# Second block: convolution sums in PSUM, weight halves subtracted on GpSimd, attention's gates between its parts, other lane rates

## The chip, the cores and the metric

The kernel runs on one core of a Trainium2 chip. The metric is the time of one execution on the device in microseconds (us); lower is better. The engines are called by their names; in the rows PE is TensorE (PEld its weight loads), DVE is VectorE, ACT is ScalarE, POOL is GpSimd and SP is SyncE, which only issues DMAs here.

## The reference, cut to what matters

Two layers of a first model run, then one layer of a second model, on 512 tokens of width 1024, all in float32. The part of the reference that the change touches is the second model's mixer:

```python
h = rms_norm(x, pre_norm1[l]) * (1.0 + sc1) + sh1
proj = h @ w_in[l]                       # 1024 x 7168: u_glu, q, k, v, gates
...
ua, ub = jnp.split(u_glu, 2, axis=-1)
u = ua * jax.nn.sigmoid(ub)
u = lax.conv_general_dilated(u, conv_w, ..., padding=[(30, 0)], feature_group_count=1024) + conv_b
u = jax.nn.silu(layer_norm(u, conv_ln_g, conv_ln_b))
y_conv = u @ conv_w_out + conv_b_out
...
att = causal_diff_attention(q1, q2, k1, k2, v, lam)     # 8 heads, v of width 128
y_att = (rms_norm(att, head_norm) * (1.0 - lam_init)).reshape(B, T, 1024)
g_conv, g_att = jnp.split(jax.nn.sigmoid(gate_logits), 2, axis=-1)
y = (g_conv * y_conv + g_att * y_att) @ w_o
x = x + g1 * rms_norm(y, post_norm1)
```

The convolution is causal, per channel, with 31 taps over 512 positions.

## The kernel before

**Weights and products.** All weights lie in one stream, cut into units of at most 128 x 1024 numbers in the order of use (`UNITS`). `unit` keeps three units ready; `_fetch` loads a unit into one of three `raw` buffers and `split` makes an upper half `wh` (a ScalarE copy that rounds) and a lower half `wl` = raw - wh (a VectorE subtraction, L380) from it. Some units are held in slots in place of the rings, as two tiles of 512 columns. Every product is three matmuls (`mm3`, L462 to L464): upper with upper, upper with lower, lower with upper. `fm` makes 128 output columns of a layer from a unit (24 matmuls of 512 columns); one `beat` follows each `mm3` there, and every third beat is a `tick`.

**Lanes.** Work that isn't on the main line is written as generators in lanes. At each tick a lane gains its rate as credit, and each whole credit runs one step, up to the next `yield`. `finish` runs a lane to its end at once. The Tile framework puts the instructions of TensorE, VectorE, ScalarE and GpSimd into an order of its own from the order of the program and its estimates, and adds the semaphores; DMAs keep the order written. Each engine then executes in order.

**Memory.** 78 slots of 128 x 512 float32 in SBUF (`big`) and eight banks of PSUM (`psum`) are handed out in the order in which they came free.

**The second block's mixer.** Eight pairs of GLU units give `us[i]`. `convolve(i)` starts `acc` in a slot on ScalarE and adds 30 taps on VectorE (`scalar_tensor_tensor`, L398), three to a step. After all eight, `conv_norm` (L1750 on) takes the mean, subtracts it in 8 steps, takes the reciprocal deviation (`sums` L589, `powm` on GpSimd L593, `spread` L619), and finishes the tiles `cn[i]` in 8 more. Both are in the lane `conv`. The main line runs four attention parts: q and k of two heads (four banks, 96 matmuls of 512 columns), `rope2`, v (two units). After each, `diff_attention` queues a transposing generator (L1663) and four blocks (`_diff_block`) in the lane `att`, two active at a time: scores L1691, masked copy L544, exponentials, transposes L1715, products L1723, head norm with a power on GpSimd, transposes L1741 into `ya`. A gate is one unit and its tanh; `combine` multiplies a finished `ya` with its gate. `GATES` says how many gates follow each part: none, none, none, sixteen. Then comes `finish("conv")`, and eight units of conv_w_out, which need all `cn`; when a `ya` isn't done there, `finish("att")` is called. The next stage is w_o, in halves of 256 columns.

Rates before: `conv` 0.6 during the GLU and the parts, 0.8 from part 3's end; `att` 1.0, and 1.5 from conv_w_out on.

## Time and profile before

| | us |
|---|---|
| median of three runs | 2490.43 (2488.10 to 2490.53) |
| profiled execution | 2488.26 |
| its span, first to last instruction | 2486.1 |
| TensorE busy | 2444.6 |
| VectorE busy | 1638.6 |
| ScalarE busy | 1064.8 |
| GpSimd busy | 318.7 |

The span holds 12206 matmuls and some 5900 instructions of VectorE, ScalarE and GpSimd. Matmuls overlap, and their ends are modelled, so that a busy TensorE isn't one at its peak: the number of matmuls in a stretch tells more. Idle time of an engine that doesn't set the pace costs nothing. PEclk is the share of TensorE's full clock that was granted.

### The profile page before, as it was taken

What the parts mean: (1) busy time and instruction counts of PE and PEld (TensorE: products, weight loads), DVE (VectorE), ACT (ScalarE), POOL (GpSimd) and SP (SyncE); (2) the same over time, 40 slices, a digit from 0 to 9 for tenths busy, and PEclk for the clock granted to TensorE, in tenths of its full rate; (3) what the DMA queues carried; (4) which work ended last, traced back from release to release, by engine and by line L of the source; (5) the groups of instructions that cost most, each with busy time, mean ns of one, the idle gap of its engine ahead of it and who ended that gap; (6) DMA issues with size and microseconds to landing.
All of it is one profiled execution on the core that took longest, in us unless ns stands there. A gap on an engine that the chain in (4) does not pass through costs nothing.

```text
span 2486.1 us, 32470 instructions
## 1 busy us (share of the span) xinstructions
PE 2444.6 (98%) x12206; PEld 2053.9 (83%) x12206; DVE 1638.6 (66%) x3064; ACT 1064.8 (43%) x1984; POOL 318.7 (13%) x820
## 2 busy tenths in 40 slices
PE   9999999999999999999999999999999989999998
PEld 7888888888888888888888788988887769988887
DVE  6998755444355488865677644799899675643335
ACT  6567433332234365643423223523445565634222
POOL 7923000000056054100000000000000000000000
PEclk9999999999999999999999999999999989999999
DMA  4222232222323322133466633322211113122232
GB/s 156 86 71 77 80 132 93 96 100 94 101 97 128 97 73 75 60 102 127 133 219 207 222 113 107 126 89 103 77 60 68 47 64 119 69 93 89 94 106 76
DMA packets 83677, 256.57 MB, mean 103 GB/s; under 512 B 9536, under 2 KB 10944, under 8 KB 83520
## 3 DMA queue, kind: packets, MB, share of 16 engines
q1 hardware_dynamic: 83520, 254.50, 30.2%
q8 instruction: 95, 1.56, 0.3%
q14 instruction: 62, 0.51, 0.1%
HBM read 248.18 MB, written 6.29 MB: 102 GB/s over the span
## 4 chain that ended last, share of the span: by engine, by line
PE 83%; DVE 7%; DMA 5%; ACT 2%; issue 2%; SPq 0%; POOL 0%; DVEq 0%; POOLq 0%; ACTq 0%
PE bank L462 26%; PE bank L463 26%; PE bank L464 26%; DMA slot<-in_wada_dram 4%; DVE slot L380 2%; DVE wl L380 2%; ACT slot L377 2%; DVE slot L398 2%; PE bank L1691 1%; PE bank L1723 1%; DMA raw<-in_w_dram 0%; PE bank L1194 0%; PE bank L1206 0%; DVE slot L394 0%; PE bank L1014 0%
## 5 line engine op out<-in xcount | busy, mean ns | idle before, releaser
L462 PE MATMUL bank<-slot,wh 128*128 128x512 f32 x2456 | 964.5, 394 | 7.3 <-ACT slot L377 7.3
L464 PE MATMUL bank<-slot,wl 128*128 128x512 f32 x2456 | 959.7, 392 | 2.8 <-DVE wl L380 2.8
L463 PE MATMUL bank<-slot,wh 128*128 128x512 f32 x2456 | 959.9, 391 | 0.0
L377 ACT ACTIVATE wh<-raw 128x1024 fp32r<-128x1024 f32 (+3 forms) x369 | 385.2, 1045 | 774.2 <-PE bank L463 401.8
L380 DVE TENSOR_TENSOR wl<-raw,wh 128x1024 fp32r<-128x1024 f32 (+3 forms) x369 | 450.4, 1221 | 216.9 <-ACT wh L377 214.9
L462 PEld LDWEIGHTS bank<-slot,wh 128*128 128x128 f32 x2456 | 463.5, 189 | 105.8 <-ACT slot L377 9.1
L464 PEld LDWEIGHTS bank<-slot,wl 128*128 128x128 f32 x2456 | 462.5, 188 | 102.8 <-DVE wl L380 6.0
L463 PEld LDWEIGHTS bank<-slot,wh 128*128 128x128 f32 x2456 | 463.2, 189 | 95.3 <-DVE slot L398 0.7
L380 DVE TENSOR_TENSOR slot<-bank,slot 128x512 f32<-128x512 f32 (+4 forms) x340 | 197.4, 592 | 229.3 <-PE bank L464 207.9
L377 ACT ACTIVATE slot<-slot 128x512 fp32r<-128x512 f32 (+4 forms) x378 | 207.6, 558 | 293.6 <-DVE slot L380 269.8
L380 DVE TENSOR_TENSOR slot<-slot,slot 128x512 f32<-128x512 f32 (+4 forms) x480 | 288.4, 619 | 50.2 <-ACT slot L377 47.1
L377 ACT ACTIVATE slot<-bank 128x512 f32<-128x512 f32 (+7 forms) x398 | 182.7, 475 | 128.2 <-PE bank L464 47.8
L463 PE MATMUL bank<-wl,slot 128*128 128x512 f32 (+1 forms) x480 | 180.9, 377 | 0.0
L464 PE MATMUL bank<-wh,slot 128*128 128x512 f32 (+1 forms) x480 | 180.1, 376 | 0.0
L462 PE MATMUL bank<-wh,slot 128*128 128x512 f32 (+1 forms) x480 | 179.5, 377 | 0.0
L463 PE MATMUL bank<-slot,slot 128*128 128x256 f32 (+1 forms) x624 | 178.3, 291 | 0.3 <-DVE slot L398 0.3
L464 PE MATMUL bank<-slot,slot 128*128 128x256 f32 (+1 forms) x624 | 178.3, 290 | 0.0
L398 DVE SCALAR_TENSOR_TENSOR slot<-slot,slot 128x512 f32<-128x512 f32 (+1 forms) x184 | 123.9, 689 | 81.1 <-DMA slot<-in_wada_dram 58.0
L462 PE MATMUL bank<-slot,slot 128*128 128x256 f32 (+1 forms) x624 | 176.5, 292 | 0.3 <-ACT slot L377 0.3
L398 DVE SCALAR_TENSOR_TENSOR slot<-slot,cw,slot 128x485 f32<-128x485 f32 (+28 forms) x240 | 166.6, 731 | 1.9 <-ACT slot L377 1.1
L380 DVE TENSOR_TENSOR slot<-slot,bank 128x512 f32<-128x512 f32 (+1 forms) x104 | 66.2, 644 | 128.8 <-PE bank L464 128.5
L463 PEld LDWEIGHTS bank<-slot,slot 128*128 128x128 f32 x624 | 118.9, 192 | 2.6 <-DVE slot L398 0.5
(197 smaller groups left out, 2163.2 us busy)
## 6 DMA issues: line engine op xcount, KB each, us to landing
raw<-in_w_dram SPq DMA_DIRECT2D x373, 512.0 KB, 3.3
slot<-in_wada_dram SPq DMA_DIRECT2D x96, 256.0 KB, 5.0
raw<-in_w_dram SPq DMA_DIRECT2D x32, 448.0 KB, 3.4
slot<-in_x_dram SPq DMA_DIRECT2D x16, 256.0 KB, 3.8
xd<-slot SPq DMA_DIRECT2D x16, 256.0 KB, 3.8
slot<-xd SPq DMA_DIRECT2D x16, 256.0 KB, 3.6
out_dram<-slot SPq DMA_DIRECT2D x8, 256.0 KB, 2.0
slot<-in_bc_dram SPq DMA_DIRECT2D x8, 128.0 KB, 3.1
```

Of the source, the lines that this page charges most:

```text
L377: return self.nc.scalar.activation(out=out, in_=in_, func=func, scale=scale, **kw)
L380: return (eng or self.nc.vector).tensor_tensor(out=out, in0=a, in1=b, op=op)
L398: return self.nc.vector.scalar_tensor_tensor(out=out, in0=a, scalar=s, in1=b, op0=op0, op1=op1, **kw)
L462: t.matmul(ps, ah, bh, start=start, stop=False)
L463: t.matmul(ps, ah, bl, start=False, stop=False)
L464: t.matmul(ps, al, bh, start=False, stop=stop)
L1691: nc.tensor.matmul(ps[e][:, :w], qk[s][x][rows, tn], qk[2 + s][y][rows, :w], start=i == 0, stop=i == 2)
L1723: nc.tensor.matmul(po[:, e], at[e][:, b], vv[b // 2][:, b % 2, 128 * e:128 * e + 128], start=b == 0, stop=b == n)
```

## The change

The convolution's running sum moves from a slot to a PSUM bank; at its end ScalarE copies it into a slot, and the sum over channels reads the bank. GpSimd makes the lower halves of the units of w_in_2 from the seventh on and of conv_w_out_2 (`BESIDE`). Two gates follow part 1, two part 2 and twelve part 3, in the order `GATE_ORDER`, where m < 8 are attention's gates and m >= 8 the convolution's. In a `_diff_block` the step ends move: one after both transposes, one after both products, one between the power on GpSimd and the product that reads it; `dfin` gets a third buffer. The lane `att` has the rate 1.45 throughout; `conv` gets its rate anew at each part from the steps that are left (`steps`), five ticks for the rest after part 3, and `conv_norm` sets 0.7.

```diff
-R1, R2, R3, R4, R5, R6 = 0.9, 1.0, 0.6, 0.6, 0.8, 1.5
+R1, R2, R3 = 0.9, 1.45, 0.6
...
-GATES = (0, 0, 0, 16)
+GATES = (0, 2, 2, 12)
+GATE_ORDER = (0, 1, 2, 3, 4, 5, 8, 9, 10, 11, 12, 13, 14, 15, 6, 7)
...
-    gates = [("w_in_2", 0, 0, 8, c + 128 * m, 128) for c in (6144, 5120) for m in range(8)]
+    gates = [("w_in_2", 0, 0, 8, (6144 if m < 8 else 5120) + 128 * (m % 8), 128) for m in GATE_ORDER]
...
+_SECOND = len(UNITS) - len(_units_second())
+BESIDE = {i for i, u in enumerate(UNITS) if i >= _SECOND + GLU_HELD and u[0] in ("w_in_2", "conv_w_out_2")}
...
-    def split(self, hi, lo, src, scale=None):
+    def split(self, hi, lo, src, scale=None, eng=None):
         if scale is None:
             self.act(hi, src)
-            self.sub(lo, src, hi.bitcast(F32))
+            self.sub(lo, src, hi.bitcast(F32), eng)
...
+        eng = self.nc.gpsimd if i in BESIDE else None
...
-                self.split(h, l, raw[:, c].rearrange("p (k c) -> p k c", k=n))
+                self.split(h, l, raw[:, c].rearrange("p (k c) -> p k c", k=n), eng=eng)
...
-                self.split(h[:, c], l[:, c], raw[:, c])
+                self.split(h[:, c], l[:, c], raw[:, c], eng=eng)
...
         def convolve(i):
-            acc = self.big(f"acc{i}")
+
+            acc = self.psum(f"acc{i}")
...
                 if j % 3 == 0:
+                    steps[0] -= 1
                     yield
             self.free(us[i])
-            conv.append(acc)
+            conv.append(self.big(f"conv{i}"))
+            self.act(conv[i], acc)
             if i == 1:
                 csum.append(self.big("csum"))
-                self.add(csum[0], conv[0], conv[1])
+                self.add(csum[0], conv[0], acc)
             elif i > 1:
                 self.add(csum[0], csum[0], acc)
+            self.free(acc)
...
+        steps = [80]
...
-        self.lane("conv", 1, R4)
         for part in range(4):
+
+            cl.rate = steps[0] / (16 * (4 - part) + 8 / 3 * (6 - sum(GATES[:part])))
...
-                self.lane("conv", 1, R5)
-            for m in range(sum(GATES[:part]), sum(GATES[:part + 1])):
+                cl.rate = steps[0] / 5
+            for m in GATE_ORDER[sum(GATES[:part]):sum(GATES[:part + 1])]:
                 gate(m)
         self.free(hs, self.cs2)
         self.finish("conv")
-        self.lane("att", 2, R6)
...
             self.act(at[e][:, :n + 1], pt[:, :n + 1])
             self.free(pt, pp[e])
-            yield
+        yield
...
             self.free(at[e])
-            if e == 0:
-                yield
-        fin = self.small("dfin", (128, 2), bufs=2)
+        yield
+        fin = self.small("dfin", (128, 2), bufs=3)
...
         self.powm(ss, ss, 2)
+        yield
         self.mul(ss, ss, fin)
...
         while len(conv) < 8:
             yield
+        self.lanes["conv"].rate = 0.7
```

## Rows read from the trace of the kernel before

**Rows 1.** The page: engines (busy us, share, instructions); a costly group (busy, mean ns).
```profile
PE 2444.6 (98%) x12206; PEld 2053.9 (83%) x12206; DVE 1638.6 (66%) x3064; ACT 1064.8 (43%) x1984; POOL 318.7 (13%) x820
...
L398 DVE SCALAR_TENSOR_TENSOR slot<-slot,cw,slot 128x485 f32<-128x485 f32 (+28 forms) x240 | 166.6, 731 | 1.9 <-ACT slot L377 1.1
```

**Rows 2.** Busy time by stretch: PE, PEld, DVE, ACT, POOL; PEclk; DMA share, GB/s.
```profile
1500.00:1550.00 50.00, 50.00 (x222) 41.42 (x221) 22.94 (x31) 14.76 (x21) 0.00 (x0) 1.00 0.35 111
1640.00:1720.00 80.00, 80.00 (x387) 67.31 (x386) 79.10 (x117) 25.66 (x34) 0.00 (x0) 1.00 0.33 112
...
1920.00:1940.00 20.00, 17.33 (x79) 12.84 (x77) 17.73 (x42) 9.29 (x26) 0.00 (x0) 0.91 0.16 53
1940.00:1980.00 40.00, 39.99 (x190) 30.33 (x188) 24.03 (x57) 22.92 (x56) 1.39 (x2) 1.00 0.21 72
1980.00:1990.00 10.00, 8.10 (x58) 6.18 (x56) 6.24 (x19) 7.38 (x23) 2.37 (x3) 1.00 0.02 4
1990.00:2000.00 10.00, 3.96 (x19) 2.90 (x18) 10.00 (x21) 10.00 (x19) 0.00 (x0) 0.66 0.00 0
2000.00:2010.00 10.00, 9.35 (x28) 7.25 (x29) 9.20 (x25) 7.37 (x22) 0.00 (x0) 0.66 0.38 131
2010.00:2060.00 50.00, 49.94 (x222) 37.41 (x222) 32.22 (x68) 26.24 (x61) 1.39 (x2) 1.00 0.26 92
2060.00:2070.00 10.00, 8.60 (x64) 7.40 (x63) 7.04 (x16) 7.32 (x19) 0.69 (x1) 1.00 0.36 133
...
1640.00:2000.00 360.00, 348.50 (x1821) 283.79 (x1819) 314.81 (x614) 164.80 (x368) 11.56 (x13) 0.99 0.21 73
```

**Rows 3.** TensorE's waits from 1980 to 2002: us in total, times, longest.
```profile
PE bank L1691 <- DVE slot L380: 3.6, 2, 2.7
...
PE bank L1691 <- DVE dmx L544: 0.8, 1, 0.8
```

**Rows 4.** Timeline of TensorE, 1982 to 2004: start, us, what, idle before.
```profile
1982.90 0.95 PE L589 MATMUL bank<-ones,slot 128*128 128x1 f32 x8
...
2000.65 1.65 PE L462 MATMUL bank<-slot,wh 128*128 128x512 f32 x3 [0.97 <-ACT slot L377]
```

**Rows 5.** VectorE's groups by shape from 1440 to 2100: busy us, mean ns.
```profile
L380 DVE TENSOR_TENSOR wl<-raw,wh 128x1024 fp32r<-128x1024 f32 x62 | 75.7, 1221 | 13.7 <-ACT wh L377 13.1 <-PE bank L464 0.6
L380 DVE TENSOR_TENSOR slot<-slot,slot 128x512 f32<-128x512 f32 x69 | 46.1, 688 | 0.4 <-ACT slot L377 0.2
L380 DVE TENSOR_TENSOR slot<-raw,slot 128x512 fp32r<-128x512 f32 x56 | 37.6, 687 | 13.7 <-ACT slot L377 12.1 <-PE bank L1715 1.3
...
L380 DVE TENSOR_TENSOR slot<-bank,slot 128x512 f32<-128x512 f32 x14 | 9.7, 692 | 40.2 <-PE bank L464 40.2
```

**Rows 6.** Timeline of GpSimd, 204 to 207 us.
```profile
204.42 0.45 POOL L380 TENSOR_TENSOR slot<-s_xx 128x128 f32<-128x128 f32 x1
...
206.42 0.73 POOL L380 TENSOR_TENSOR slot<-s_xx 128x256 f32<-128x256 f32 x1
```

**Rows 7.** GpSimd's groups by shape, whole span.
```profile
L593 POOL TENSOR_TENSOR dss<-dss,mhalf 128x2 f32<-128x2 f32 x16 | 13.4, 835 | 446.6 <-DVE dss L395 249.6 <-ACT djk L377 197.0
```

**Rows 8.** Timeline of VectorE and GpSimd, 755 to 760 us.
```profile
755.80 3.42 DVE L380 TENSOR_TENSOR wl<-raw,wh 128x896 fp32r<-128x896 f32 x1
...
756.36 0.30 POOL L380 TENSOR_TENSOR s_w<-slot,s_lr 128x64 f32<-128x64 f32 x1
...
758.13 1.23 POOL L380 TENSOR_TENSOR s_w<-slot,s_lr 128x64 f32<-128x64 f32 x1
```

**Rows 9.** Two lines' instructions: count, duration in ns min/median/max, first and last start.
```profile
L1168 DVE COPY slot<-slot x64: 260/270/1452, 42.8 to 1013.6; 32x128 f32<-32x128 f32 x64
...
L1248 DVE COPY slot<-bank x64: 372/384/400, 123.2 to 1069.3; 32x128 f32<-32x128 f32 x64
```

**Rows 10.** Timeline of VectorE, 1901 to 1905 us.
```profile
1901.14 3.96 DVE L398 SCALAR_TENSOR_TENSOR slot<-slot,cw,slot 128x505 f32<-128x505 f32 x6
```

## The prediction

> **What bounds the kernel now.** I read the page first. TensorE is busy 98% of the span [rows 1], so work that leaves another engine is worth nothing by itself: only stretches in which TensorE idles or runs slowly can pay. Next came the busy time by stretch. Where nothing disturbs it, TensorE issues 222 matmuls of 512 columns in 50 us, 0.225 us each [rows 2]. The second block's convolution and attention lie between about 1640 and 2070 us, and there the reader sees two different things [rows 2]. From 1640 to 1720 VectorE is full (79.1 of 80 us) while TensorE loses nothing. From 1920 on TensorE loses: 2.67 us idle at 1920 to 1940, then 1.90, 6.04 and 0.65 us in the three stretches from 1980 to 2010, and 1.40 us at 2060 to 2070. Between the two, at 1940 to 1980, VectorE is busy only 24.0 of 40 us. So the work is badly spread: too much early, too little at 1940, too much at once at 1990, where VectorE and ScalarE are both busy 10.00 of 10 us.
>
> The waits say what the big gap is: attention's score matmuls (L1691) wait for a difference on VectorE (L380), 2.7 us at the longest [rows 3]. The timeline shows the chain: the sums over partitions (L589) that conv_norm needs before its last eight steps run only at 1982.90, and conv_w_out's first matmul (L462) starts at 2000.65, after a wait for ScalarE [rows 4]. In the ten us from 2000 only 28 matmuls start, where 44 would at 0.225 us. [...]
>
> Why conv_norm is late can be counted in the code. A tick is three beats, one beat is three matmuls of 512 columns, so a tick lasts 9 x 0.225 = 2.0 us plus what the lanes put in. The convolutions take 8 x 10 = 80 steps, conv_norm 17. Ten GLU units give 26.7 ticks x 0.6 = 16 steps, four parts 64 x 0.6 = 38, sixteen gates 42.7 x 0.8 = 34: 88 of 97. The other 8 or 9 are drained by `finish("conv")`, and the late sums fit that. Attention has 4 x 32 = 128 steps; 48 + 42.7 ticks at rate 1.0 do 91, conv_w_out's 21.3 ticks at 1.5 another 32, the rest is drained at the end: the idle at 2060.
>
> **What the change can take away.** Idle at 1980 to 2010: 1.90 + 6.04 + 0.65 = 8.6 us. Low clock after it: 16 missing matmuls x 0.225 = 3.6 us less the 0.65 us already counted, 3.0 us. At 1920 to 1940: 2.67 us idle and, with the granted clock at 0.91, 0.09 x 20 = 1.8 us, together 4.5 us; VectorE was nearly full there (17.7 of 20). At 2060: 1.4 us. Sum 17.5 us.
>
> **The change part by part.** *Rates and gates.* By the same count the convolution has 64 steps left at part 0 and 64 + 16 ticks to do them in, rate 0.8, and stays there; in part 3 some 4 steps remain, done in 5 ticks; conv_norm's 17 steps at 0.7 take 24 of the 27 ticks left in the last twelve gates. So `finish("conv")` finds nothing. Attention gets 16 x 3 + 5.3 x 2 + 32 = 90.7 ticks x 1.45 = 131 steps for 128, and is done before conv_w_out. The number of matmuls and of weight transfers stays. Thus the gap, its low clock and the idle at 2060 go, if the other engines follow.
>
> *GpSimd takes the lower halves.* 58 units from the seventh GLU unit on; of these, 42 whole ones and 16 half tiles of attention's values fall between 1640 and 2000. VectorE loses 42 x 1.221 + 16 x 0.687 = 62 us there [rows 5]. Undelayed, GpSimd's instructions with two inputs take 0.45 us for 128 columns and 0.73 us for 256 [rows 6], 2.2 ns a column, so 0.73 + 768 x 0.0022 = 2.4 us for 1024. Without any fixed part it would be 4 x 0.73 = 2.9 us; I take 2.4. A unit lasts TensorE 24 x 0.225 = 5.4 us and is fetched two units ahead, so either value is hidden; the cover is gone above 5.4 us. [...]
>
> GpSimd's queue is in order, and its power for the head norm (835 ns [rows 7]) now stands behind a 2.4 us subtraction. VectorE's next product waits for it, and behind that product all of VectorE. The new yield puts the product about two lane steps later, 2 / 1.45 ticks x 2 us = 2.8 us against up to 3.2: at worst 0.4 us for each of 16 blocks. conv_norm's own power has no such yield: up to 2.4 us once, in front of its `spread`.
>
> *Sharing with VectorE.* At 755.80 a VectorE subtraction of 896 columns took 3.42 us, where 1.221 x 896 / 1024 gives 1.07. Meanwhile GpSimd's instructions ran at their normal 0.30 us, up to one that took 1.23 us in the same form when VectorE at last ran [rows 8]. So one excludes the other. A copy on VectorE from SBUF has a median of 270 and a maximum of 1452 ns; the same from PSUM, in the same stages, 384 and 400 [rows 9]. Hence the convolution's instructions, with the sum in PSUM, should run beside GpSimd, and those with two SBUF inputs should not. [...]
>
> Its price here: in 1640 to 2000 VectorE is busy 314.8 us. Less 62, plus at most the 32.2 us that it does at 2010 to 2060 and that now comes earlier [rows 2]: 285 us. The stretch shrinks to about 360 - 18 = 342 us, so 57 us are free. GpSimd would be busy 42 x 2.4 + 16 x 1.3 = 121 us, 35% of it. VectorE comes to some 104 runs of instructions with two SBUF inputs there (16 rope groups, 3 runs in each of 16 attention blocks, about 32 in conv_norm, 8 combines); 104 x 0.35 x half of 2.4 us = 44 us. Bounds: nothing, and all 121. I take 44: VectorE is then busy 329 of 342 us, which just fits.
>
> *Sums in PSUM.* No row shows VectorE writing PSUM. Reading it costs nothing: 512 columns take 692 ns from PSUM and 688 ns from SBUF [rows 5]. Bounds: none, or the loss of the overlap by which six convolution instructions of 0.73 us [rows 1] take 3.96 us, 0.65 us apart [rows 10]: 0.08 x 240 = 19 us of VectorE. I take none, since reading shows none. Eight ScalarE copies lie beside units of 5.4 us, hidden: ScalarE was under half busy at 1920 to 1940. One bank of eight is gone, so while four banks hold q and k, attention turns over three, not four.
>
> *New waits.* Head norms 16 x 0.4 x 0.35 = 2.2 us, conv_norm's power 2.4 x 0.35 = 0.8 us: 3.0 us. Lower bound 0; the upper ends are the rivals.
>
> Net 17.5 - 3.0 = 14.5 us. The profiled execution took 2488.3 us, 2.2 us more than its span; it becomes 2473.8. The median of the runs is 2490.4, 2.1 us above the profiled one, so **2476 us**.
>
> **The rivals.** *VectorE still sets the pace.* If each of the 58 GpSimd instructions costs VectorE 1.2 us, not 0.76, that is 70 us against 57 free: 13 us too many, the drain comes back in part, gain 4, 2486 us. For it: VectorE was held over 2 us in [rows 8]. Against: half of its time is convolution, which should be immune. *A bank too few, slower.* With three banks, each of the 32 score steps takes the banks of the step before, about one lane step earlier, and TensorE, in order, waits until VectorE's masked read is done. The nearest row is the 0.8 us wait for dmx [rows 3]; 32 x 0.8 = 26 us against 17.5 gained: 2498 us. It decides above 17.5 / 32 = 0.55 us a step. For it: VectorE is nearly full. Against: matmuls of the parts can be put in front of the scores. *Everything fits.* No new waits; the low clock of 1990 to 2000 goes too (at most 0.34 x 10 = 3.4 us, not counted above because TensorE was mostly idle), and that stretch's 19 small matmuls shrink from 3.96 / 19 = 0.21 us each to the 8.10 / 58 = 0.14 us of the ten us before, 1.3 us [rows 2]: 17.5 + 4.7 = 22.2 us, 2468 us.
>
> **How the numbers follow.** Forecast 0.55, everything fits 0.10, VectorE sets the pace 0.20, a bank too few 0.15. The range reaches from 2 us below the best case, whose clock terms are estimates, to midway between the two bad ones: 2466 to 2492; the forecast's own is 2470 to 2482. About 5 us (0.2%) can be told from no change: faster takes the forecast, the best case and under half of the pace rival, 0.73; same 0.12; slower 0.15, the bank rival.
>
> **What would show it.** Right: conv_norm's second sums (L589) well before the last gate, no idle of several us and no low clock before conv_w_out, VectorE even between 1700 and 2000, 66 GpSimd subtractions of 2 to 3 us, products with two SBUF inputs above their 688 ns, convolution instructions still near 0.73 us. Wrong: GpSimd subtractions above 5 us; convolution instructions stretched too; conv_w_out's first matmuls still waiting for ScalarE; score matmuls waiting for VectorE time after time.

## The result, and the profile after

The changed kernel takes 2520.82 us (median of four runs, 2519.07 to 2525.02) against 2489.26 us for the kernel before in the same comparison: a ratio of 1.0129, 95% interval 1.0116 to 1.0142. It is slower, by 31.6 us, and lies above the range of 2466 to 2492 and above the slow rival's 2498. The profiled execution took 2519.07 us, with a span of 2517.3.

Three lines of the page of the changed kernel: the engines, the convolution's group, GpSimd's new group.

```profile
PE 2454.1 (97%) x12206; PEld 2062.8 (82%) x12206; DVE 1636.5 (65%) x2998; ACT 1069.4 (42%) x1992; POOL 463.2 (18%) x886
...
L404 DVE SCALAR_TENSOR_TENSOR bank<-slot,cw,bank 128x493 f32<-128x493 f32 (+14 forms) x240 | 173.7, 735 | 7.0 <-ACT bank L383 2.9
L386 POOL TENSOR_TENSOR wl<-raw,wh 128x1024 fp32r<-128x1024 f32 x50 | 127.1, 2547 | 221.7 <-ACT wh L383 212.3
```

Against [rows 1] TensorE has the same 12206 matmuls, and a tap of the convolution costs VectorE 735 ns in place of 731. GpSimd's subtraction takes 2.55 us where 2.4 was estimated. So the parts have about the forecast prices. But VectorE's total hardly falls, 1638.6 to 1636.5 (1646.8 in the run below that leaves the subtractions on VectorE): nearly all of what it gave away it got back in longer instructions.

Most of the loss has one place. It lies between the first matmul of the first part's q and k and the first of w_o: 1689.7 to 2066.1 before, 1693.0 to 2096.0 after, nearly the same work (1881 and 1893 matmuls). The next two fences are these two stretches (columns as in [rows 2]), first of the kernel before, then of the changed one.

```profile
1689.70:2066.10 376.40, 362.79 (x1881) 291.19 (x1880) 312.13 (x649) 190.82 (x447) 12.95 (x15) 0.98 0.21 72
```

```profile
1693.00:2096.00 403.00, 370.67 (x1893) 300.80 (x1892) 315.00 (x602) 199.13 (x467) 130.73 (x71) 0.94 0.20 71
```

It is 26.6 us longer, of the 31.2 us by which the span grew; 3.3 us lie ahead of it, where the runs below differ by more among themselves (the stretch starts at 1689.2 to 1700.6), and 1.3 behind it. TensorE idles 403.0 - 370.7 = 32.3 us against 13.6, which is 18.7 us; the other 7.9 us are busy time, 370.7 against 362.8, at a granted clock of 0.94 against 0.98. "The stretch" below is always this one, read in the same way.

Stretches of 20 us in the changed kernel show where, same columns:

```profile
1800.00:1820.00 20.00, 20.00 (x107) 16.73 (x106) 6.04 (x12) 8.79 (x23) 8.73 (x8) 1.00 0.16 54
1820.00:1840.00 20.00, 12.33 (x60) 9.51 (x59) 18.29 (x36) 10.04 (x25) 7.53 (x3) 0.76 0.44 157
1840.00:1860.00 20.00, 16.48 (x110) 14.72 (x110) 19.52 (x46) 6.90 (x25) 1.23 (x2) 0.90 0.00 1
...
1900.00:1920.00 20.00, 13.44 (x61) 9.39 (x59) 19.96 (x43) 9.90 (x24) 8.39 (x4) 0.81 0.45 158
...
2000.00:2020.00 20.00, 20.00 (x81) 15.21 (x79) 4.90 (x21) 7.30 (x21) 4.08 (x3) 0.80 0.00 1
```

The gap at the drain is gone: while the second sums of conv_norm run (2007.4 to 2011.7) TensorE is busy all the time, where [rows 2, 4] had 6.04 us idle in 10. The granted clock there is still low, 0.80. In place of the gap stand new stalls at the ends of the parts' q and k. VectorE is little used in one stretch (6.04 of 20 us) and nearly full in the next two (18.29, then 19.52): the evenness that the forecast wanted did not come.

TensorE's waits in the changed kernel, 1440 to 2140 (total, times, longest), are what the forecast named as a sign that it is wrong, score matmuls that wait for VectorE. Line numbers have moved: here L1703 are the scores, L551 is the masked read (it writes `dmx`), L1727 the transposes behind the difference (L404), L1735 the products, L1753 the last transposes, L469 to L471 `mm3`, L386 the plain two-input instructions and L383 ScalarE's. In the other runs the same lines lie a few numbers off.

```profile
PE bank L1703 <- DVE dmx L551: 16.8, 6, 5.9
PE bank L1727 <- DVE slot L404: 4.9, 2, 3.2
PE bank L1753 <- ACT slot L383: 3.7, 3, 1.9
PE bank L1735 <- ACT slot L383: 3.1, 3, 1.5
```

The longest one in the timeline, TensorE first, then VectorE, then GpSimd:

```profile
1824.57 0.39 PE L471 MATMUL bank<-wh,slot 128*128 128x512 f32 x1
1824.88 2.40 PE L1703 MATMUL bank<-slot,slot 64*128 64x128 f32 x18
1833.13 1.21 PE L1703 MATMUL bank<-slot,slot 64*128 64x128 f32 x6 [5.86 <-DVE dmx L551]
1836.04 1.65 PE L1703 MATMUL bank<-slot,slot 64*128 64x512 f32 x3 [1.69 <-DVE dmx L551]
1837.62 0.58 PE L469 MATMUL bank<-slot,slot 128*128 128x256 f32 x1
```

```profile
1820.25 0.69 DVE L386 TENSOR_TENSOR slot<-bank,slot 128x512 fp32r<-128x512 f32 x1 [1.05 <-ACT slot L383]
1822.22 10.65 DVE L386 TENSOR_TENSOR slot<-slot,slot 128x256 f32<-128x256 f32 x9 [1.28 <-ACT slot L383]
1832.79 0.28 DVE L551 CUSTOM_DVE_ANT_0 slot<-bank,slot 128x128 f32<-128x128 f32 x1
```

```profile
1817.17 2.38 POOL L386 TENSOR_TENSOR wl<-raw,wh 128x1024 fp32r<-128x1024 f32 x1 [7.14 <-ACT wh L383]
1824.12 7.53 POOL L386 TENSOR_TENSOR wl<-raw,wh 128x1024 fp32r<-128x1024 f32 x3 [4.58 <-ACT wh L383]
```

Right behind part 2's q and k TensorE has eighteen score matmuls in a row, three steps' worth, and then needs the banks that the masked reads (L551) must free. These stand on VectorE behind nine rope instructions, which take 10.65 us while three GpSimd subtractions run back to back for 7.53 us. The matmuls of v (L469, 256 columns) are behind the scores in TensorE's queue, so nothing fills the wait. It looks like a tale of GpSimd; the experiments say otherwise, since the stalls stay when GpSimd's part is undone.

### The profile page after: what moved, and what is told of

It reads as the page before. It is cut to its first block, busy times and chain, and to the rows that moved or that the text cites. A ratio compares the mean times of both kernels' runs of the same rounds, so it can differ in the third digit from the quotient of the medians.

```text
span 2517.3 us, 32504 instructions
## 1 busy us (share of the span) xinstructions
PE 2454.1 (97%) x12206; PEld 2062.8 (82%) x12206; DVE 1636.5 (65%) x2998; ACT 1069.4 (42%) x1992; POOL 463.2 (18%) x886
## 4 chain that ended last, share of the span: by engine, by line
PE 76%; DVE 11%; DMA 6%; issue 2%; ACT 2%; POOL 2%; SPq 1%; DVEq 0%; POOLq 0%; ACTq 0%
PE bank L469 23%; PE bank L470 23%; PE bank L471 23%; DVE slot L386 4%; DMA slot<-in_wada_dram 4%; DVE wl L386 2%; DVE slot L404 2%; ACT slot L383 2%; PE bank L1703 1%; DMA raw<-in_w_dram 1%; POOL s_w L386 1%; POOL slot L386 1%; PE bank L1735 1%; DVE bank L404 1%; DVE slot L400 0%
## 5 line engine op out<-in xcount | busy, mean ns | idle before, releaser
L469 PE MATMUL bank<-slot,wh 128*128 128x512 f32 x2456 | 964.3, 394 | 5.5 <-ACT slot L383 5.5
L471 PE MATMUL bank<-slot,wl 128*128 128x512 f32 x2456 | 960.5, 392 | 4.3 <-DVE wl L386 4.3
L383 ACT ACTIVATE wh<-raw 128x1024 fp32r<-128x1024 f32 (+3 forms) x369 | 385.1, 1044 | 744.0 <-PE bank L470 356.1
L471 PEld LDWEIGHTS bank<-slot,wl 128*128 128x128 f32 x2456 | 462.9, 188 | 106.2 <-DVE wl L386 9.3
L469 PEld LDWEIGHTS bank<-slot,wh 128*128 128x128 f32 x2456 | 463.3, 189 | 101.6 <-ACT slot L383 5.9
L386 DVE TENSOR_TENSOR wl<-raw,wh 128x1024 fp32r<-128x1024 f32 (+3 forms) x319 | 389.2, 1221 | 204.1 <-ACT wh L383 202.5
L386 DVE TENSOR_TENSOR slot<-bank,slot 128x512 f32<-128x512 f32 (+4 forms) x340 | 197.5, 591 | 242.5 <-PE bank L471 208.6
L383 ACT ACTIVATE slot<-slot 128x512 fp32r<-128x512 f32 (+4 forms) x378 | 207.3, 558 | 315.5 <-DVE slot L386 291.2
L386 DVE TENSOR_TENSOR slot<-slot,slot 128x512 f32<-128x512 f32 (+4 forms) x473 | 299.5, 652 | 62.9 <-ACT slot L383 58.9
L383 ACT ACTIVATE slot<-bank 128x512 f32<-128x512 f32 (+7 forms) x406 | 187.5, 476 | 131.9 <-PE bank L471 47.4
L404 DVE SCALAR_TENSOR_TENSOR slot<-slot,slot 128x512 f32<-128x512 f32 (+1 forms) x184 | 129.9, 723 | 89.3 <-DMA slot<-in_wada_dram 60.6
L469 PE MATMUL bank<-slot,slot 128*128 128x256 f32 (+1 forms) x624 | 180.7, 296 | 2.9 <-ACT slot L383 2.2
L471 PE MATMUL bank<-slot,slot 128*128 128x256 f32 (+1 forms) x624 | 181.0, 293 | 0.0
L470 PE MATMUL bank<-slot,slot 128*128 128x256 f32 (+1 forms) x624 | 180.2, 293 | 0.3 <-DVE slot L404 0.3
L469 PE MATMUL bank<-wh,slot 128*128 128x512 f32 (+1 forms) x480 | 179.9, 379 | 0.5 <-ACT slot L383 0.5
L471 PE MATMUL bank<-wh,slot 128*128 128x512 f32 (+1 forms) x480 | 180.3, 376 | 0.0
L404 DVE SCALAR_TENSOR_TENSOR bank<-slot,cw,bank 128x493 f32<-128x493 f32 (+14 forms) x240 | 173.7, 735 | 7.0 <-ACT bank L383 2.9
L386 POOL TENSOR_TENSOR wl<-raw,wh 128x1024 fp32r<-128x1024 f32 x50 | 127.1, 2547 | 221.7 <-ACT wh L383 212.3
L386 DVE TENSOR_TENSOR slot<-slot,bank 128x512 f32<-128x512 f32 (+1 forms) x111 | 71.0, 646 | 133.9 <-PE bank L471 128.3
```

What stands on the lines that cost most here:

```text
L383: return self.nc.scalar.activation(out=out, in_=in_, func=func, scale=scale, **kw)
L386: return (eng or self.nc.vector).tensor_tensor(out=out, in0=a, in1=b, op=op)
L404: return self.nc.vector.scalar_tensor_tensor(out=out, in0=a, scalar=s, in1=b, op0=op0, op1=op1, **kw)
L469: t.matmul(ps, ah, bh, start=start, stop=False)
L470: t.matmul(ps, ah, bl, start=False, stop=False)
L471: t.matmul(ps, al, bh, start=False, stop=stop)
```

## The experiments

All ratios are to the kernel before in the same session, with the 95% interval. "Behind" is the time from w_o's first matmul to the end of the span, 420.0 us before and 421.3 after. No run that does the whole work was measured faster than the kernel before.

| run | ratio | stretch | behind |
|---|---|---|---|
| the whole change | 1.0129 [1.0116, 1.0142] | 403.0 | 421.3 |
| undo_gpsimd | 1.0110 [1.0095, 1.0125] | 400.2 | 421.3 |
| undo_psum | 1.0272 [1.0255, 1.0289] | 439.9 | 424.5 |
| rates_gates | 1.0082 [1.0067, 1.0097] | 393.5 | 421.9 |
| own_bank | 1.0141 [1.0126, 1.0157] | 403.8 | 423.4 |
| att_slow | 1.0046 [1.0021, 1.0071] | 377.1 | 426.2 |
| rates_gates_slow | 1.0020 [1.0001, 1.0038] | 369.3 | 428.0 |
| rates_gates_slow5 | 1.0031 [1.0020, 1.0043] | 372.2 | 428.8 |
| att_mid | 1.0133 [1.0118, 1.0149] | 403.8 | 422.0 |
| conv_end | 1.0008 [0.9989, 1.0027] | 374.5 | 420.0 |
| gates_only | 1.0024 [1.0008, 1.0040] | 379.4 | 422.7 |
| steps_only | 1.0036 [1.0023, 1.0048] | 381.2 | 423.0 |
| gates_gpsimd | 1.0097 [1.0081, 1.0112] | 399.9 | 420.4 |
| half_taps_before | 0.9955 [0.9942, 0.9967] | 361.4 | 420.5 |
| half_taps_after | 1.0104 [1.0090, 1.0118] | 396.6 | 422.4 |
| pause | 1.0182 [1.0168, 1.0196] | 416.3 | 425.0 |
| crowd | 1.0011 [1.0002, 1.0020] | 370.4 | 427.5 |
| width_one | 1.0092 [1.0076, 1.0108] | 396.0 | 425.8 |
| width_three | 1.0058 [1.0043, 1.0074] | 388.1 | 423.0 |

### The parts undone one by one

**undo_gpsimd**: the whole change, lower halves on VectorE.

```diff
-        eng = self.nc.gpsimd if i in BESIDE else None
+        eng = None
```

> The changed kernel, with the lower halves back on VectorE. Exclusion theory (VectorE's instructions with two SBUF inputs, rope first, are held by rows of GpSimd subtractions, and the scores behind them): the waits for dmx, 16.8 us, and most of the low clock go, 2485 to 2495 us. Bank theory (the sum in PSUM takes a bank from attention and ties the start of each convolution to that bank's earlier user): the waits for dmx and the gaps of the convolution stay, 2510 us or more. Density theory (attention at 1.45 is too close for VectorE): 2510 us or more too.

Measured 1.0110. The loss stays, so GpSimd is not its main cause; the 0.19% (4.7 us) between the two runs is at the edge of the noise, for their intervals overlap. TensorE still waits for the masked reads, now also in front of the matmuls of v (1640 to 2140):

```profile
PE bank L1703 <- DVE dmx L551: 6.9, 4, 4.4
PE bank L469 <- DVE dmx L551: 6.6, 3, 3.2
```

In the stretch, VectorE by shape (busy us, mean ns), first this run, then the whole change, then GpSimd in the whole change:

```profile
L386 DVE TENSOR_TENSOR slot<-slot,slot 128x512 f32<-128x512 f32 x53 | 35.4, 683 | 2.2 <-ACT slot L383 2.1
...
L386 DVE TENSOR_TENSOR slot<-slot,slot 128x256 f32<-128x256 f32 x32 | 12.0, 419 | 0.0
```

```profile
L386 DVE TENSOR_TENSOR slot<-slot,slot 128x512 f32<-128x512 f32 x53 | 44.1, 849 | 0.6
L386 DVE TENSOR_TENSOR slot<-slot,slot 128x256 f32<-128x256 f32 x32 | 21.0, 696 | 5.0 <-ACT slot L383 4.9
...
L386 DVE TENSOR_TENSOR dss<-dss,dfin 128x2 f32<-128x2 f32 x16 | 10.0, 627 | 4.7 <-POOL dss L600 4.5
```

```profile
L386 POOL TENSOR_TENSOR wl<-raw,wh 128x1024 fp32r<-128x1024 f32 x38 | 98.3, 2592 | 146.6 <-ACT wh L383 137.2 <-PE bank L1703 9.4
L386 POOL TENSOR_TENSOR slot<-raw,slot 128x512 fp32r<-128x512 f32 x16 | 20.3, 1290 | 13.3 <-ACT slot L383 13.3
```

In this stretch 38 whole and 16 half subtractions leave VectorE, 38 x 1.222 + 16 x 0.687 = 57.4 us, but its busy time falls only from 324.5 to 315.0. So 47.9 us came back, 0.89 us for each GpSimd instruction, where the forecast had 44 us and 0.76.

**undo_psum**: the whole change with the running sum in a slot.

```diff
-            acc = self.psum(f"acc{i}")
+            acc = self.big(f"acc{i}")
...
```

> The changed kernel, with the convolution's sum back in a slot; GpSimd keeps the lower halves. Exclusion theory: now the convolution's instructions are held too, slower than the changed kernel, 2530 us or more, their mean above 0.8 us. Bank theory: the gaps between convolutions (24.6, 39.6, 15.5 and 10.0 us) close and attention has its four banks, 2490 to 2505 us. Density theory: no change, about 2520 us.

Measured 1.0272, the worst of all. With two SBUF inputs the taps are held as well, 933 ns in the mean against 735, and the transposes behind the rope wait 21.1 us at one place. The taps on the page of this run, and then TensorE's waits in its stretch:

```profile
L404 DVE SCALAR_TENSOR_TENSOR slot<-slot,cw,slot 128x511 f32<-128x511 f32 (+27 forms) x240 | 211.2, 933 | 1.1 <-ACT slot L383 0.9
```

```profile
PE bank L1673 <- DVE slot L386: 26.2, 4, 21.1
```

So the sum in PSUM does what the forecast said: it takes the convolution out of GpSimd's way.

**rates_gates**: rates, gates and step ends alone; sums in slots, VectorE for all halves (the two edits above together).

> Only gates, rates and step ends of the change; sum in a slot and lower halves on VectorE as before. Exclusion theory and bank theory: both causes are gone, 2480 to 2492 us. Density theory: still slow, 2505 us or more, with score matmuls waiting for dmx.

Measured 1.0082. Most of the loss is here, in the part that was to bring the whole gain. Its waits, 1440 to 2140, have the same two kinds as the whole change:

```profile
PE bank L1701 <- DVE dmx L551: 12.9, 6, 8.9
PE bank L1725 <- DVE slot L404: 11.8, 4, 4.1
```

The sum in PSUM added to this costs 1.0110 - 1.0082 = 0.28% (7 us, give or take 5 by the two intervals).

**own_bank**: the convolution keeps one bank throughout in place of queueing for one eight times.

```diff
+            if not own:
+                own.append(self.psum("acc"))
+            acc = own[0]
-            acc = self.psum(f"acc{i}")
...
```

> The changed kernel, but one bank is set aside for all eight convolutions, in place of a bank from the common list for each. Attention has as many banks as in the change. Bank theory, the part on ties: the gaps of the convolution close, VectorE is no longer at 6.0 of 20 us at 1800 to 1820, 2500 to 2510 us. Exclusion theory: within 5 us of the changed kernel, 2520 us, and the rope instructions still take several us.

Measured 1.0141: the gaps between convolutions close and nothing is gained. VectorE is busy 17.60 of 20 us from 1800 to 1820, where the whole change had 6.04, and yet TensorE is busy only 12.57 of 20 us in the next stretch, as in the whole change (12.33). That the convolution queues for its bank is no cost.

### Attention's rate

**att_slow**: the whole change with attention at 1.0, and 1.5 from conv_w_out on, as before.

```diff
-R1, R2, R3 = 0.9, 1.45, 0.6
+R1, R2, R3 = 0.9, 1.0, 0.6
...
         self.finish("conv")
+        self.lane("att", 2, 1.5)
```

> The changed kernel with attention's lane back at 1.0 per tick, and 1.5 from conv_w_out on. Density theory (attention at 1.45 puts more score steps in flight than VectorE can mask): the waits for dmx fall from 16.8 to under 5 us, 2490 to 2502 us. Exclusion theory alone: waits stay, 2510 us or more.

**rates_gates_slow** is the same edit on rates_gates.

> Gates, step ends and the convolution's even rate alone (sum in a slot, lower halves on VectorE), attention's lane at 1.0 as before. Density theory: back to 2480 to 2492 us, against 2508 us with 1.45. Rival, the convolution at 0.8 or the new step ends cost it: 2500 us or more.

att_slow's stretch is 377.1 us, 25.9 shorter than the whole change's; its score matmuls wait 1.4 us for dmx in place of 16.8. rates_gates_slow has 369.3 against 393.5. Part of it is given back behind the stretch (426 to 428 us in place of 421), because attention's rest then runs beside w_o. In both profiled executions the stretch also starts late, at 1700.4 and 1700.6; attention's lane only begins there, and measured again the second kernel starts it at 1693.6, so this is not the rate's doing. In ratios the rate costs 1.0129 - 1.0046 = 0.83% (21 us) with the other parts and 1.0082 - 1.0020 = 0.62% without. TensorE's wait for dmx in att_slow, 1590 to 2140:

```profile
PE bank L1704 <- DVE dmx L551: 1.4, 2, 1.0
```

**rates_gates_slow5**, the same kernel in more rounds:

> The even convolution rates, the gates between the parts and the new step ends with attention at 1.0 and 1.5, sums in slots, VectorE for the weight halves, measured again in more rounds. An earlier run gave 1.0020 [1.0001, 1.0038] beside a spread of 0.7% in the runs of before, while its stretch from part 0 to w_o was 7 us shorter than before's. If the 7 us are real, 0.997 to 0.999; if they are given back behind w_o's start, 0.999 to 1.003.

1.0031, and 372.2 us: its 4 us in the stretch are real, and more than lost again behind it. The rate without the other parts then costs 1.0082 - 1.0031 = 0.51%. The kernel beats the whole change, not the kernel before.

**att_mid**: the whole change with 1.2.

```diff
-R1, R2, R3 = 0.9, 1.45, 0.6
+R1, R2, R3 = 0.9, 1.2, 0.6
```

> The whole change with attention's lane at 1.2 throughout in place of 1.45. If the loss grows with the number of attention steps in flight, it lies between the two ends measured (1.0046 at 1.0 and 1.5, 1.0129 at 1.45): 1.006 to 1.010. If there is a point above which the lane outruns its buffers, and 1.2 lies below it, it is 1.005 or less; if the end of the lane also counts (attention drained in conv_w_out and w_o), it is under 1.004.

1.0133: as bad as 1.45, a miss for all three answers. The price does not grow from 1.2 to 1.45; it is there in full at 1.2, with other waits: 7.3 us of transposes for the difference, 6.9 of scores for dmx, 5.8 of the transposes of q and k for the rope.

### What there was to take away

**conv_end**: the kernel before with R5 at 1.05, so that by the count of steps the lane `conv` is empty at its end.

```diff
-R1, R2, R3, R4, R5, R6 = 0.9, 1.0, 0.6, 0.6, 0.8, 1.5
+R1, R2, R3, R4, R5, R6 = 0.9, 1.0, 0.6, 0.6, 1.05, 1.5
```

> The kernel before with one number changed: the convolution's lane at 1.05 in place of 0.8 from part 3's end. The prediction's account of the gap before conv_w_out: the 8 or 9 drained steps are done by then, idle at 1980 to 2010 and its low clock go, 10 to 13 us faster, about 2477 us. Rival: the same VectorE and ScalarE work only comes earlier and stalls there, within 5 us of 2489.

Measured 1.0008: no gain above 0.11% (2.7 us), the end of the interval, where the forecast's account wanted 10 us or more. The drain's idle shrinks, 1980 to 2000, from 1.90 + 6.04 = 7.9 us [rows 2] to 2.5, and 1920 to 1940 gets worse (15.45 busy, clock 0.74, against 17.33 and 0.91):

```profile
1920.00:1940.00 20.00, 15.45 (x64) 11.70 (x63) 17.54 (x46) 8.20 (x24) 0.00 (x0) 0.74 0.17 54
...
1980.00:1990.00 10.00, 10.00 (x52) 8.46 (x52) 10.00 (x16) 9.97 (x18) 0.00 (x0) 1.00 0.09 28
1990.00:2000.00 10.00, 7.53 (x47) 6.01 (x45) 7.45 (x14) 8.63 (x22) 0.70 (x1) 0.95 0.58 211
```

In the stretch TensorE idles 374.5 - 364.0 = 10.5 us in place of 13.6, at a clock of 0.97 in place of 0.98. An emptied lane mostly moves the wait; it hardly removes it.

**gates_only** (`GATES`, `GATE_ORDER` and the stream's order alone) and **steps_only** (the moved step ends and the third dfin alone), each on the kernel before:

> The kernel before with the new place and order of the gates alone; rates and step ends as before. If the gates between the parts give attention and VectorE time, 2480 to 2490 us; if they only move the drain (fewer ticks at 0.8 after part 3, about 2 convolution steps more to drain), 2490 to 2496 us; 2500 us or more if they are a cause of the loss.

> The kernel before with the moved step ends of a block of attention and the third dfin buffer alone; all rates as before. A block keeps its number of steps but the power has a step of its own. Expected 0.999 to 1.002 under either theory: it separates the step ends from the rates in the remaining loss of the kernels that run attention at 1.0.

1.0024 and 1.0036: they lose some 6 and 9 us, each by itself. Neither was costed in the forecast. Both traces show some of it at the drain: TensorE idles 12.2 us from 1980 to 2020 in gates_only (before 8.6), where the convolution has fewer ticks at 0.8, and 9.3 us from 1990 to 2010 in steps_only (before 6.7). That rates_gates_slow, which holds both and the even convolution rates, loses only 0.2 to 0.3%, speaks for a small gain by the even rates; no run has these alone.

**gates_gpsimd**: GpSimd halves the gates' and conv_w_out's units only, on the kernel before (`eng` is GpSimd for these 24 units).

```diff
...
-                self.split(h[:, c], l[:, c], raw[:, c])
+                self.split(h[:, c], l[:, c], raw[:, c], eng=eng)
```

> The kernel before with GpSimd making the lower halves of the 16 gates' and 8 conv_w_out units alone, 24 x 1.22 = 29 us less on VectorE between 1900 and 2060, where no rope and no convolution run. If VectorE's fullness makes the loss at the drain, as the run of before with half the taps showed for the whole stretch (11 us), some 3 to 6 us go: 0.998 to 0.999. If GpSimd's instructions hold conv_norm's and attention's instructions with two SBUF inputs for longer than VectorE gains: 1.000 to 1.006.

1.0097. VectorE gives away 24 x 1.22 = 29 us and yet is busy 328.3 us in the stretch against 312.1: 45 us come back, 1.9 us an instruction. The expectation was wrong that no convolution runs there: its last taps, with two SBUF inputs, are held (the shape below took 1042 ns in the mean, 725 before). All 240 taps take 182.9 us in place of 166.6, 16 of the 45 us; some 23 of the other 29 fall on further instructions with two SBUF inputs, by their means here and before (128x512: 785 against 687 ns, 999 against 686 and 875 against 746; 128x256: 557 against 420; 128x2: 428 against 157).

```profile
L400 DVE SCALAR_TENSOR_TENSOR slot<-slot,cw,slot 128x491 f32<-128x491 f32 x7 | 7.3, 1042 | 0.1
```

### A full VectorE, the place, or the distance of steps

**half_taps_before** and **half_taps_after** leave out every second tap, on the kernel before and on the whole change.

```diff
-                self.stt(acc[:, s:], us[i][:, :512 - s], self.cw[:, 31 * i + j:31 * i + j + 1], acc[:, s:], ALU.mult, ALU.add)
+                if j % 2 == 0:
+                    self.stt(acc[:, s:], us[i][:, :512 - s], self.cw[:, 31 * i + j:31 * i + j + 1], acc[:, s:], ALU.mult, ALU.add)
```

> The kernel before with every second tap of the convolution left out (15 of 30 instructions for each of the 8 tiles, 120 x 0.731 = 88 us less VectorE work between 1540 and 2000; the steps and their ticks stay, so the matmuls and the attention lane keep their places). It is the baseline for the next run. If the idle at the drain comes from VectorE's fullness, some of the 8.6 us of idle at 1980 to 2010 goes: 0.996 to 0.999 of before. If it comes from the chain sums, power, spread alone: 0.999 to 1.000.

> The whole change with the same 120 convolution instructions left out. Theory VectorE: attention at 1.45 loses because its chains meet a full VectorE at the end of each part's q and k. With 88 us less on VectorE the stalls go, the stretch from part 0 to w_o shrinks from 403 us to 380 or less, and the time is within 0.3% of the baseline's (half the taps, before). Theory banks: the score matmuls wait for PSUM banks whose release is a chain of ScalarE and VectorE latencies, whatever VectorE's load; then the stretch stays above 392 us and the time stays 0.8% or more above the baseline's.

Without half of the taps the kernel before gains 0.45% (11 us); so most of its 17.5 us hung on the convolution's work on VectorE, by the load or by the length of the chain before the drain, which this run does not tell apart. The whole change is still 2513.21 / 2475.65 = 1.0152 of that baseline: with 70 us less on VectorE in the stretch it loses at least as much to it. The stretch of half_taps_after, and its largest wait:

```profile
1692.70:2089.30 396.60, 369.52 (x1893) 302.52 (x1892) 244.82 (x510) 198.50 (x466) 132.07 (x71) 0.92 0.20 72
```

```profile
PE bank L1704 <- DVE dmx L551: 11.6, 7, 3.7
```

VectorE is busy 244.8 of 396.6 us there, and the score matmuls wait all the same. The total load is not the cause. The run does not take away the jam at one place, though: behind part 2's q and k VectorE is as full as ever. That alone is not enough either, since the kernel before has VectorE as full at the like place and TensorE busy throughout. First half_taps_after, then the kernel before:

```profile
1820.00:1840.00 20.00, 13.81 (x77) 11.39 (x76) 19.89 (x42) 7.20 (x20) 4.29 (x2) 0.74 0.24 80
```

```profile
1830.00:1840.00 10.00, 10.00 (x63) 8.46 (x62) 9.93 (x16) 6.43 (x12) 0.00 (x0) 1.00 0.56 210
1840.00:1850.00 10.00, 10.00 (x61) 8.33 (x60) 10.00 (x32) 4.17 (x15) 0.00 (x0) 1.00 0.33 107
```

**pause** (the whole change; attention at 1.8, but still from the last quarter of q and k to the middle of v) and **crowd** (the kernel before; attention at 2.0 just there and 0.5 elsewhere). The diff is pause's; crowd has 2.0 for 0, 0.5 for 1.8, and 1.0 again in the gates:

```diff
+                al.rate = 0 if i == 3 else 1.8
                 wh, wl, _ = self.unit("w_in_2")
...
+                al.rate = 0 if t < 2 else 1.8
                 if t % 2 == 0:
```

> The whole change, but attention's lane stands still from the last quarter of a part's q and k to the middle of its v (5.4 of a part's 16 ticks) and runs at 1.8 in the other ticks, so that the steps done by the end of the gates are about the same (134 against 131). Theory phase: what costs is that score steps meet the rope at the end of q and k, where four banks hold q and k and VectorE's queue has the rope ahead of the masked reads; then most of the 26 us go: 1.000 to 1.006. Theory rate: what costs is that the lane runs ahead of its buffers, wherever it does so; at 1.8 it is as bad or worse: 1.012 to 1.020.

> The kernel before with nothing changed but the place of attention's steps within a part: 2.0 a tick from the last quarter of q and k to the middle of v, 0.5 in the other ticks, mean 1.0 as before, and 1.0 again in the gates. Theory phase: score steps crowd together with the rope, TensorE waits for dmx there, 10 us or more are lost: 1.004 to 1.012. Theory rate: the mean is unchanged, so 0.999 to 1.003.

1.0182 and 1.0011, as the recorded theory of the rate had it: taking the steps away from the rope does not help while the rate elsewhere is 1.8, and putting them there costs little while the mean is 1.0. crowd even has a stretch of 370.4 us, with 31 matmuls fewer in it, and loses that behind it. TensorE idles 21.5 us in crowd's stretch (before 13.6), 10.9 of them in one wait at 2010, at the drain, and 5.9 from 1810 to 1850, the end of part 2's q and k (before 0.6). Its stretch, and its largest wait there (the transposes L1718 for the difference):

```profile
1695.20:2065.60 370.40, 348.91 (x1850) 283.29 (x1848) 309.62 (x644) 188.72 (x441) 13.78 (x15) 0.97 0.21 73
```

```profile
PE bank L1718 <- DVE slot L398: 13.0, 3, 10.9
```

In pause TensorE waits 14.8 us for the split of the transposed q and k, with VectorE full over the same stretch:

```profile
PE bank L1705 <- DVE slot L386: 14.8, 5, 5.4
```

```profile
1820.00:1840.00 20.00, 8.16 (x39) 6.35 (x38) 20.00 (x37) 6.49 (x18) 5.60 (x3) 0.63 0.23 79
```

**width_one** (the kernel before, one attention block active) and **width_three** (the whole change, three active, and six dmx tiles in place of four). The diff is width_one's, which has 1 in the later rate of the lane too:

```diff
-        al = self.lane("att", 2, R2)
+        al = self.lane("att", 1, R2)
```

> The kernel before with one attention block active at a time in place of two, rates as before. A block's next step then follows its last after one step of the lane (2.0 us at rate 1.0) in place of two (4.0 us); in the whole change at 1.45 it is 2 x 2.0 / 1.45 = 2.8 us, at 1.2 it is 3.3 us. Theory latency: a block's step needs the result of the one before through VectorE and ScalarE, and TensorE's queue is in order, so what costs is the short distance between two steps of a block; at 2.0 us it is worse than the whole change: 1.012 to 1.030. Theory rate as such (work of the lane per stretch, banks, VectorE's load at a moment): the number of steps per tick is as before, and one block holds fewer banks: 0.998 to 1.004.

> The whole change with three attention blocks active in place of two, and two more dmx buffers. The distance of two steps of a block is then 3 x 2.0 / 1.45 = 4.1 us, as in the kernel before. Theory latency: most of the 26 us go, 1.000 to 1.006. Theory banks: three blocks want more of the seven banks at a time while q and k hold four of them, 1.013 to 1.030.

1.0092 and 1.0058. One block at the old rate loses most of what the whole change loses; three at the new rate win back 0.71% of its 1.29%. That is the order of the theory of distance, against the rival in both runs, but not its size: width_one should have been worse than the whole change. TensorE's two largest waits, 1590 to 2140, first width_one, then width_three:

```profile
PE bank L1741 <- ACT slot L377: 10.9, 3, 5.7
PE bank L462 <- ACT slot L377: 8.9, 2, 8.6
```

```profile
PE bank L1727 <- DVE slot L404: 16.5, 5, 6.9
PE bank L469 <- ACT slot L383: 3.6, 3, 1.4
```

With one block its last transposes (L1741) wait for the scaled copy that comes behind the power, 5.7 us at 1818 and 3.3 at 1869; the 8.6 us of L462 are at conv_w_out's first matmul, the drain, where the kernel before waits 0.97 us [rows 4]. The drain as a whole idles TensorE 11.7 us (1990 to 2050), 8.6 before, so most of width_one's 16.6 us of further idle lies ahead of it. With three, the waits for dmx are gone, and the transposes (L1727) wait for the difference on VectorE.

## Why the prediction was wrong

**The step that failed: rates and gates.** The forecast counted that 90.7 ticks at 1.45 do 131 steps for 128, and then let the faster lane cost nothing, "if the other engines follow". They don't: attention's rate alone costs 0.51 to 0.83%, 13 to 21 us, by ratios (1.0082 against 1.0031, 1.0129 against 1.0046). The reading that fits most of the runs is one of distance. A block's next step uses what its last one left on VectorE and ScalarE. With two blocks active and a tick of 2.0 us, two steps of a block are, by this estimate, 2 x 2.0 / 1.0 = 4.0 us apart before, 2.8 at 1.45 and 3.3 at 1.2. TensorE executes in order, and a score or transpose that is not ready holds the main line behind it (scores 5.86 us at 1833.13, with the matmuls of v behind them; transposes up to 6.9 us in width_three). Shown: the price hangs on the rate (att_slow, rates_gates_slow), is there at 1.2 (att_mid), does not hang on VectorE's total load (half_taps_after), and does not go when the steps leave the rope (pause). A loss of like size comes at the old rate with one block active (width_one), and the whole change loses less than half as much with three (width_three). That the distance is the reason is argued, not shown. Against it stand att_mid, which costs as much as 1.45; width_one, which costs less although its distance of 2.0 us is the shortest, and some 3 us of whose idle are the drain's; and crowd, which has the same 2.0 us in a third of each part's ticks and loses little. How much of width_three is its two more dmx tiles is open. So is a rival that no run tests: every edit also gives the Tile framework another program to order, and part of each difference may be that order.

**What the change can take away: the 17.5 us were not there to take.** The idle at the drain went, as counted (no stall at the sums, [rows 4] against 2007.4 in the changed kernel). But conv_end, which shrinks it to a third by one number, gains nothing that can be told from the noise: TensorE waits at other places. Of what was tried, only less work on VectorE frees it (half_taps_before, 11 us for 88 us of taps), and the change took off just 9.5. Nor did the low clock go, the forecast's 3.0 us: the granted clock, 0.66 from 1990 to 2010 before [rows 2], is 0.80 from 2000 to 2020 in the changed kernel, where TensorE is busy all the time. Low clock and idle stand together in several stretches (0.76 beside 12.33 us busy of 20 from 1820); that the one comes of the other was the author's estimate, and no run isolates it.

**Step ends and gates at nothing.** They were moved without a price; steps_only and gates_only cost 0.36% and 0.24%. For the step ends the reason is open. A head's transposes now stand one step before the products that read them, where they stood two before, but in steps_only the products (L1723) wait for ScalarE only 1.9 us in all, against 2.5 before; its longest wait is 4.9 us of a score matmul for VectorE at the drain.

**GpSimd and VectorE.** Nearly right in size: 2.55 us where 2.4 was taken, 47.9 us given back where 44 was taken, taps in PSUM at 735 ns. That a run of VectorE instructions waits for half a subtraction was the author's estimate; no run shows the half, only the sum. Nor does the number of SBUF inputs tell alone what is held: the copies from SBUF in [rows 9] have one, and six of them took 4.62 us from 203.97 on, beside the GpSimd instructions of [rows 6], where 270 ns each would be 1.6. In the changed kernel taps with one SBUF input and their sum in PSUM are not held (735 against 731 ns), 128x512 instructions with two SBUF inputs are (849 against 683). While three subtractions ran from 1905.15 to 1913.14, two taps took 0.72 us each, and the three 128x512 instructions with two SBUF inputs that began beside them 2.27, 2.62 and 1.66 us. The new waits behind the head norms' power, 2.2 of the 3.0 us, did not come as waits: in front of the product that reads the power VectorE stands idle 4.7 us in all, 5.2 before. The 9.5 us that remain buy nothing here; the part costs 0.19%, at the edge of the noise, and with sums in slots 1.0272 - 1.0082 = 1.9%.

**Sum in PSUM at nothing.** For VectorE, yes. For the kernel it costs 0.28%, some 7 us, with GpSimd out of play. One bank less for attention is the likely reason; no run isolates it.

**The rivals.** "A bank too few" came nearest: the sign, the place (score matmuls waiting for dmx), and a loss. But its cause explains at most those 7 us, since with no bank given to the convolution rates_gates still loses 0.82%; and the waits are six of up to 5.9 us, not 32 of 0.8. "VectorE still sets the pace", as a matter of its total work, falls with half_taps_after. One sum of the whole, in the order of the runs: 0.31% for gates, step ends and even rates, 0.51 for attention's rate, 0.28 for the sum in PSUM, 0.19 for GpSimd, together 1.29%; another order of undoing would give other shares.

## What to carry to other kernels

The rate of a background lane can have a ceiling that a count of steps does not show: at 1.45 TensorE waited 16.8 us for masked reads in front of the scores, 2.1 before. Here 1.2 already cost the full price, and three chains in place of two won back more than half; so estimate the time between two steps of a chain beside its way through the other engines, and try the number of chains before the rate. An idle gap before a drain is not yet a gain; change the one number that closes it, and look whether the time moves, before planning on it. And moving work to GpSimd is to be counted together with what VectorE's instructions with two SBUF inputs lose by it (here 47.9 of 57.4 us came back), not by what leaves VectorE alone.

## What the runs showed of the hardware

GpSimd subtractions that run back to back held VectorE over several instructions: nine rope instructions took 10.65 us while three subtractions ran for 7.53 us, where 9 x 419 ns (undo_gpsimd) would be 3.8 us. Even the 128 x 2 product behind the power took 627 ns in the mean, where it had 155 in undo_gpsimd and 157 before:

```profile
L380 DVE TENSOR_TENSOR dss<-dss,dfin 128x2 f32<-128x2 f32 x16 | 2.5, 157 | 5.2 <-POOL dss L593 5.2
```

What one GpSimd subtraction cost VectorE differed here with the place of the taps' sum. Over the whole span 66 of them take 50 x 1.222 + 16 x 0.687 = 72 us off VectorE. With the sum in slots its busy time still rises by 31.7 us (undo_psum 1669.4, rates_gates 1637.7), so that 1.6 us come back for each; with the sum in PSUM it falls by 10.3 (1646.8 to 1636.5), so that 0.94 us come back.

VectorE writing PSUM, which no row showed before: a tap that reads and writes its sum there took 735 ns in the mean, one with its sum in a slot 731 in the kernel before [rows 1].
